# A state-space layer's weighted sums moved out of its opening, one weight split moved behind the products, and one sum moved out of the first FFN unit

## The chip, the cores and the metric

The program runs on one core of a Trainium2 chip. A core has five engines with a queue of instructions each: TensorE (PE in the profile, with its weight loads as PEld), VectorE (DVE), ScalarE (ACT), GpSimd (POOL) and SyncE (SP, which here only issues transfers). Each works its own queue in order and waits at an instruction until what it needs has been signalled. Transfers between device memory (HBM) and on-chip memory run on 16 DMA engines, and are issued from the queues of SP, ACT and POOL.

The metric is the time of one execution on the device, in microseconds (us); the figure for a kernel is the median over its runs. Before the change it is 1346.33 us.

## The reference

The model is a trunk of two layers over 512 positions of width 1024, in float32. Each layer has a token mixer and then a gated feed-forward network (FFN), both between RMS norms; a conditioning vector `c` gives each of the four sub-layers a shift, a scale and a gate (adaLN).

```python
mod = (jax.nn.silu(c) @ ada_w + ada_b).reshape(bsz, DEPTH, 2, 3, D_MODEL)
for i in range(DEPTH):
    shift, scale, gate = (mod[:, i, 0, k][:, None, :] for k in range(3))
    h = rmsnorm(x, norm_g[i, 0]) * (1.0 + scale) + shift
    y = short_conv_mixer(...) if i % 2 == 0 else ssd_mixer(...)
    x = x + gate * rmsnorm(y, norm_g[i, 1])
    shift, scale, gate = (mod[:, i, 1, k][:, None, :] for k in range(3))
    h = rmsnorm(x, norm_g[i, 2]) * (1.0 + scale) + shift
    x = x + gate * rmsnorm(swiglu_ffn(h, f_w_in[i], f_w_out[i]), norm_g[i, 3])
```

So `ada_w` is a matrix of 1024 x 12288, and `mod` is a vector of 12 pieces of 1024 numbers. A piece is needed only when its sub-layer uses it. The mixer of the second layer is a state-space layer (Mamba-2):

```python
z, xbc, dt_raw = jnp.split(h @ w_in, [M_D_INNER, M_D_INNER + M_CONV_DIM], axis=-1)
xbc = silu(causal_depthwise_conv(xbc, conv_w) + conv_b)      # x, B and C of 8 groups
dt = softplus(dt_raw + dt_bias)                              # 512 x 32 heads
cs = cumsum(dt * a)                                          # within a chunk
y = ssd_chunked(xs, dt, a, bm, cm) + d_skip * xs             # in chunks, per group
y = rms_normalize(y * silu(z), per group) * norm_g
return y @ w_out
```

## The kernel before, in words

**Number format.** TensorE is fed with pairs: a float32 weight tile is split into a rounded part (a copy on ACT) and the remainder (a subtraction on DVE, lines 230 and 231, tiles `whl`), and each product is three matmuls (lines 285 to 287). A split of a 128x1024 tile therefore costs one instruction on ACT and one on DVE, and PE can use the tile only after both.

**Order of work.** In the parts that the change touches, the order on PE, ACT and DVE is written out by hand (`tc.manual_schedule`): the instructions stand on each engine in the order in which the code issues them. In the first FFN, SP's and POOL's order is written by hand as well; in the state-space layer SP's is left to a scheduler.

**AdaLN's sums.** A piece of `mod` is summed on DVE from eight row blocks of `ada_w`: a block of 128x1024 (512 KB) is loaded into a tile `ada_st` and added to `ada_acc`, scaled by silu(c). The first block of a piece is line 125, the other seven are line 127; then line 140 folds the sum (`ada_fold`), PE adds over partitions with one small matmul (line 147, `ada_ps`), and DVE writes `mods` (line 151 and one of 156 or 158). This work is cut into steps and strewn over the program between other work. In the first FFN, `sums(n)` takes `n` steps of the three pieces that are summed there. For the last four pieces the generator `late_sums` (line 1870) yields 36 steps (eight sums and a fold, four times), and `late(n)` takes `n` of them. After each sum it issues the load of the block three further on (line 1879). `late_fin` takes a piece whose fold is done through its matmul and its last additions, one stage per call.

The tiles of these loads come from a pool `ysp` of five buffers. One holds the accumulator; one is taken in turn by `sqs`, the squares of a group's output, which PE reads at the group's end (line 1857, `ssg`); three are left for blocks that wait to be summed.

**The state-space layer** starts from PE's six leading products (`li`): the raw dt, and x, B, C and z of group 0. From the raw dt a chain runs through `dt_steps`: PE turns it (line 1618, `tokT`), DVE copies it (1619), ACT takes an exponential (1622, 1623), DVE forms softplus in fifteen small instructions (1626 to 1636), and PE forms the cumulative sums (1640, `cumT`). Behind `cumT` on PE stands everything else of the layer.

Then the groups follow. A pass of the loop `for g in range(1, NG - 1)` finishes group g (`cur`), while PE makes the products of group g + 1 (`nxt`) and the weights of group g + 2 (`nn`) are fetched. I call these passes 1 to 6, and the block ahead of them pass 0. In one pass PE does: `ssg` of the group before, two products of `nxt` (24 matmuls each, `ip`), the transposes and small products of `step_a` (`xtok`, `btokp`, `cb`), a product, the states (`st`), a product, `step_cc` (`yo`, then `yd` in two halves), and two products of z. DVE does: the head (`late_fin`, then `late`), `prev.norm` (line 1868, which needs ACT's `rg`), the taps of four convolutions (1676, three each), six weight splits (231), `step_a` (1743, 1745, 1757), the decays (1799), the chain of states `prev` (1777, 1779), and `step_cc` (1827 to 1830, for two halves). `nxt.later[i]` is a pair of functions, the ACT part and the DVE part of a weight tile's split: 0 and 1 are x, 2 is B, 3 is C, 4 and 5 are z. PE uses tile 5 in the second product of z, after `step_cc`.

PE's `yo` reads `prev`, and `st` reads `xw` (line 1743). PSUM has four `aux` banks, which `st`, `yo`, `yd`, `ssg` and the small products of `late_fin` take in turn.

**The first FFN** makes most of its inner products in 12 units (`Units`, seven quarter products per unit, tiles `sA`, `sB`, `sC` on line 654). In each unit DVE and ACT copy results out, split weights and take one step of `sums`. In the last stage of that FFN, passes `k` of a loop make plain products and take one more step each, up to `k0 + 4`.

Of the kernel before, what the change touches and what calls it, by code (L numbers as in the profile page):

```python
# [38 lines left out]
def trunk_kernel(  # L39
# [249 lines left out]
    def mm_chunk(pst, w, h, sl=FULL, ks=range(KD)):  # L289
        for k in ks:  # L290
            mm3(pst[:, sl], w, k, h[k], sl, k == 0, k == KD - 1)
# [402 lines left out]
    class Values:  # L694
# [27 lines left out]
        def sums(self, b):  # L722
            va, vb, k, (lo, hi) = self.va, self.vb[b], self.half[b], HALVES
            dve.tensor_tensor(va[:, k, hi], vb[:, :, hi], va[:, k, hi], SUB)
            dve.tensor_add(vb[:, :, hi], vb[:, :, hi], va[:, k, lo])
# [26 lines left out]
    with ExitStack() as ph:  # L752
# [582 lines left out]
        with tc.manual_schedule(engines={PE_ENGINE, mybir.EngineType.SP, mybir.EngineType.Activation,  # L1335
# [51 lines left out]
            for u in range(UN1):  # L1387
                v = u - 1
                end = u == UN1 - 1
                if not end:  # L1390
                    un.fetch(u + 2)
                else:
                    more_n = load_w([(f_w_in[0], (fu + 1) * P, P), (f_w_in[0], DFF + fu * P, P)], later=splits)
                un.product(u, "P1")
                if u:
                    un.c12(v)
                else:
                    up(3, acc[1])
                un.split_x(u + 1)
                if u:  # L1400
                    un.product(v, "P7")
                un.keep(u, "A", 0, lo_)
                un.product(u, "P5")
                if u:
                    un.c22(v)
                low_parts(1)
                un.product(u, "P2")
                un.keep(u, "C", 1, hi_)
                if u:
                    un.product(v, "P4")  # L1410
                un.c11(u)
                for step in todo:
                    next(step, None)
                sums(1)
                un.split_z(u)
                if not end:
                    un.sum_y(u + 1)
                    un.sum_s(u + 1)
                un.product(u, "P6")
                if u:  # L1420
                    un.c21(v)
                if end:
                    for op in splits[2]:
                        op()
                    more_n += load_w([(f_w_in[0], DFF + (fu + 1) * P, P)], later=splits)
                else:
                    un.split_y(u + 1)
                un.product(u, "P3")
                un.keep(u, "A", 0, hi_)
                if not end:  # L1430
                    un.split_s(u + 1)
# [53 lines left out]
            for k in range(k0, last + 1):  # L1485
                if k - k % 2 + 4 <= last:
                    load_pair_at(k - k % 2 + 4, k % 2)
                if k < k0 + 6:
                    for i in (0, 2):
                        x_load((k - k0) % 3, i + (k - k0) // 3)  # L1490
                if k in (last - 2, last - 1):
                    xy_load(n_s - 2 + k - last + 2)
                tiles[k] = in_chunk(ws[k], h)
                for step in todo:
                    next(step, None)
                q, j = divmod(k - 3, 4)
                if j < 2:
                    gate(4 + 2 * q + j, tiles[k - 1])
                else:
                    up(2 + 2 * q + j, tiles[k - 1])  # L1500
                for op in splits.get(k + 2, ()):
                    op()
                low_parts()
                sums(1 if k < k0 + 5 else 0)
                if k == 2 * NF - 12:
                    ggs.append(make_gg(1, gg_tile))
                if k == last - 1:
                    assert next(madds, 0) == 0 and not ada_sets and not quarters
                    sums_p.close()
                    ph.enter_context(tc.tile_pool(name="gap", bufs=1, side="right", reuse_waits="tile")).tile(  # L1510
                        [P, 216], F32, tag="gap", name="gap")
                    ao_p.append(ph.enter_context(tc.tile_pool(name="aop", bufs=3, side="right", reuse_waits="tile")))
                    ao_p[0].tile([P, 2, 2, 256], F32R, tag="ao", name="ao")
                    gotp = ph.enter_context(tc.tile_pool(name="gotp", bufs=1, side="right", reuse_waits="tile"))
                    c22 = gotp.tile([P, 2, T], F32, tag="c22", name="c22")
                if k >= last - 1:
                    w_prep(seq[k - last + 1])
                    a_prep(seq[k - last + 1])
# [65 lines left out]
    with ExitStack() as ph:  # L1584
# [285 lines left out]
        def late_sums():  # L1870

            uh = tmp.tile([P, 256], F32, tag="uh", name="four", bufs=2)
            sets, st = (64, 72, 80, 88), []

            def load(n):
                if n < KD * len(sets):
                    q0, k = sets[n // KD], n % KD
                    st.append(flat(ysp.tile([P, 2, T], F32, tag="ys", name="ada_st")))
                    dma(st[n], ada_w[k * P:(k + 1) * P, q0 * P:q0 * P + D])

            acc = flat(ysp.tile([P, 2, T], F32, tag="ys", name="ada_acc"))
            for n in range(3):
                load(n)
            yield uh[:, 0:P]
            for i, q0 in enumerate(sets):
                for k in range(KD):
                    ada_madd(acc, st[i * KD + k], k)
                    load(i * KD + k + 3)
                    yield
                part = uh[:, P + 32 * (i % 2):P + 32 * (i % 2) + 32]  # L1890
                ada_fold(acc, part)
                fins_late.append(late_end(q0, part))
                yield
# [8 lines left out]
        def late(n):  # L1902
            for _ in range(n):
                next(steps_late, None)
# [30 lines left out]
        with tc.manual_schedule(engines={PE_ENGINE, mybir.EngineType.Activation, mybir.EngineType.DVE}):  # L1935
            cur, nxt, nn = Group(0), Group(1), Group(2)
            nxt.weights(0)
            steps_late = late_sums()
            four = next(steps_late)
            make_four(four)  # L1940
            convs = [cur.conv(i, lead_ps[1 + i]) for i in range(4)]
            late(4)
            rest(0)
            raw = dt_raw(lead_ps[0])
            rest(1)
# [20 lines left out]
            for i in range(3):  # L1966
                next(convs[i])
            nxt.weights(1)
            mm_chunk(pz, wz1[0], h, ks=range(2, KD))
            next(convs[3])  # L1970
            for i in range(2):
# [49 lines left out]
            for g in range(1, NG - 1):  # L2021
                prev, cur, nxt = cur, nxt, nn
                nn = Group(g + 2) if g + 2 < NG else None
                nxt.e, nxt.ecs = decays(g + 1)
                conv2 = [nxt.project(i) for i in range(2)]
                prev.root()
                late_fin()
                late(4)
                nxt.later[3][0]()
                prev.norm()  # L2030
                next(conv2[0])
                next(conv2[0])
                cur.e_sub(0)
                nxt.later[3][1]()
                nxt.weights(2)
                nxt.later[4][0]()
                next(conv2[1])
                cur.e_sub(1)
                late(1)
                cur.step_a()  # L2040
                for q in range(2):
                    cur.e_exp(q)
                next(conv2[1])
                for q in range(2):
                    cur.e_mul(q)
                next(conv2[0])
                nxt.later[4][1]()
                nxt.later[5][0]()
                conv2.append(nxt.project(2))
                next(conv2[2])  # L2050
                cur.states()
                next(conv2[1])
                next(conv2[2])
                nxt.later[5][1]()
                conv2.append(nxt.project(3))
                next(conv2[3])
                next(conv2[2])
                if nn:
                    nn.weights(0)
                    nn.later[0][0]()  # L2060
                late_fin()
                cur.step_cc()
                next(conv2[3])
                if nn:
                    nn.later[0][1]()
                    nn.split(1)
                next(conv2[3])
                cur.split_sq()
                nxt.project_z(0)
                if nn:  # L2070
                    nn.weights(1)
                    nn.split(2)
                else:
                    for op in next(parts[0]):
                        op()
                nxt.project_z(1)
                cur.sums()
# [485 lines left out]
```

## Time and profile before

| what | value |
|---|---|
| median of 3 runs | 1346.33 us (1344.09 to 1349.07) |
| the profiled execution | 1343.74 us, of which the span of the profile is 1342.0 us |
| PE busy | 1309.1 us, 98% of the span |
| DVE busy | 1022.0 us, 76% |
| ACT busy | 721.3 us, 54% |
| DMA | 234.87 MB, 175 GB/s on average |

A busy share is taken over the whole program; the waits that count lie in single places. Two views matter most here: the waits (who waited for whom, how long) and the timeline of single engines. A row of the timeline gives the start in us, the time, the engine, the line, the operation, the tiles as out<-in, and in brackets the idle time before it with what ended that idle time. A matmul's time in a row reaches from its start to its end; matmuls overlap, so the pace of PE is read from the distance of two starts.

### The profile page before, as it was taken

How to read it: one execution, taken by the hardware profiler on the slowest of the kernel's cores; microseconds unless marked ns; L12 is line 12 of the kernel's file. 1: busy time of each engine (PE TensorE's matmuls, PEld its weight loads, DVE VectorE, ACT ScalarE, POOL GpSimd, SP SyncE). 2: the span in 40 equal slices, each digit the busy share in tenths (PEclk: the TensorE clock that was granted, in tenths of full speed). 3: DMA queues.
4: the chain of work that ended last, by engine and by line, in shares of the span. 5: the costliest groups of instructions: out<-in, count | busy, mean ns of one | idle time of the engine just before them, and what ended most of it. 6: DMA issues, size and time to landing. Idle time of an engine off the chain costs nothing.

```text
span 1342.0 us, 20442 instructions
## 1 busy us (share of the span) xinstructions
PE 1309.1 (98%) x7869; PEld 1150.1 (86%) x7869; DVE 1022.0 (76%) x1533; ACT 721.3 (54%) x1258; POOL 109.3 (8%) x135
## 2 busy tenths in 40 slices
PE   8999999999999999968999999999999999999998
PEld 7788889899988888867888888888789999998886
DVE  5577767888875886738889889787577777776888
ACT  5333355455423666626666677566475454554665
POOL 0000000121100320000000000000000111100330
PEclk9999999999999999988999999999999999999999
DMA  9767651799867866144654656423341888868871
GB/s 310 236 213 236 224 169 40 199 255 250 219 209 273 191 122 161 32 142 145 213 162 138 195 188 204 126 95 98 107 149 28 201 198 215 214 172 283 191 134 63
DMA packets 224277, 234.87 MB, mean 175 GB/s; under 512 B 10148, under 2 KB 176948, under 8 KB 223156
## 3 DMA queue, kind: packets, MB, share of 16 engines
q1 hardware_dynamic: 203856, 191.03, 45.9%
q0 software_dynamic: 16176, 29.63, 12.7%
q10 hardware_dynamic: 4148, 12.90, 2.9%
q8 instruction: 62, 1.02, 0.3%
q14 instruction: 35, 0.29, 0.1%
HBM read 201.66 MB, written 2.24 MB: 152 GB/s over the span
## 4 chain that ended last, share of the span: by engine, by line
PE 83%; DVE 7%; DMA 3%; ACT 3%; issue 2%; SPq 2%; DVEq 0%; ACTq 0%
PE sA L654 10%; PE ip L285 10%; PE ip L287 10%; PE ip L286 10%; PE y L387 7%; PE sC L654 5%; PE cA L2271 4%; PE cA L1310 3%; PE li L285 2%; PE li L287 2%; PE li L286 2%; PE sB L654 2%; DMA ada_st<-in_ada_w_dram 2%; PE li L936 1%; DVE whl L617 1%
## 5 line engine op out<-in xcount | busy, mean ns | idle before, releaser
L285 PE MATMUL ip<-h,whl 128*128 128x512 f32 x648 | 256.7, 396 | 0.2 <-DVE cv L1036 0.2
L287 PE MATMUL ip<-h,whl 128*128 128x512 f32 x648 | 252.9, 390 | 0.0
L286 PE MATMUL ip<-h,whl 128*128 128x512 f32 x648 | 252.8, 390 | 0.0
L285 PEld LDWEIGHTS ip<-h,whl 128*128 128x128 f32 x648 | 122.2, 189 | 26.4 <-issue 2.0
L287 PEld LDWEIGHTS ip<-h,whl 128*128 128x128 f32 x648 | 121.9, 188 | 25.8
L286 PEld LDWEIGHTS ip<-h,whl 128*128 128x128 f32 x648 | 122.2, 189 | 24.4
L654 PE MATMUL sA<-tq,whl 128*128 128x256 f32 x1008 | 131.5, 284 | 2.2 <-ACT g L664 1.2
L654 PEld LDWEIGHTS sA<-tq,whl 128*128 128x128 f32 x1008 | 125.3, 192 | 4.2 <-DVE g L681 2.1
L127 DVE SCALAR_TENSOR_TENSOR ada_acc<-ada_st,csil,ada_acc 128x1024 f32<-128x1024 f32 x70 | 89.7, 1281 | 19.2 <-DMA ada_st<-in_ada_w_dram 18.4
L231 DVE TENSOR_TENSOR whl<-wst,whl 128x1024 fp32r<-128x1024 f32 x70 | 84.8, 1219 | 22.0 <-ACT whl L230 22.0
L617 DVE TENSOR_TENSOR whl<-wsu,whl 128x1024 fp32r<-128x1024 f32 x58 | 70.8, 1221 | 33.3 <-ACT whl L616 33.3
L387 PE MATMUL y<-whlo,ys 128*128 128x512 f32 x384 | 89.3, 392 | 0.0
L387 PEld LDWEIGHTS y<-whlo,ys 128*128 128x128 f32 x384 | 71.8, 188 | 15.8 <-issue 0.6
L285 PE MATMUL li<-h,whl 128*128 128x256 f32 x288 | 83.3, 289 | 0.0
L287 PE MATMUL li<-h,whl 128*128 128x256 f32 x288 | 81.5, 283 | 0.0
L286 PE MATMUL li<-h,whl 128*128 128x256 f32 x288 | 81.4, 283 | 0.0
L230 ACT CAST whl<-wst 128x1024 fp32r<-128x1024 f32 x70 | 72.7, 1040 | 2.2 <-DMA wst<-in_m_w_in_dram 2.2
L1229 POOL DMA_DIRECT2D sg<-sg x28 | 24.6, 877 | 539.3 <-DMA sg<-in_f_w_in_dram 322.5
L616 ACT CAST whl<-wsu 128x1024 fp32r<-128x1024 f32 x58 | 60.6, 1045 | 13.3 <-PE sB L654 13.3
L1676 DVE SCALAR_TENSOR_TENSOR cu<-ip,cols,cu 128x511 f32<-128x511 f32 (+2 forms) x84 | 62.7, 746 | 3.9 <-ACT cu L1673 1.8
L2271 PE MATMUL cA<-whlo,ao 128*128 128x512 f32 x264 | 61.0, 390 | 0.4 <-DVE w2h L2478 0.2
L2271 PEld LDWEIGHTS cA<-whlo,ao 128*128 128x128 f32 x264 | 49.3, 188 | 11.6 <-ACT whlo L2236 1.2
(381 smaller groups left out, 2657.4 us busy)
## 6 DMA issues: line engine op xcount, KB each, us to landing
ada_st<-in_ada_w_dram SPq DMA_DIRECT2D x96, 512.0 KB, 6.2
wsu<-in_f_w_in_dram SPq DMA_DIRECT2D x30, 512.0 KB, 5.7
sg<-in_f_w_in_dram SPq DMA_DIRECT2D x56, 256.0 KB, 3.5
wsu<-in_f_w_in_dram SPq DMA_DIRECT2D x56, 256.0 KB, 4.8
wst<-in_m_w_in_dram SPq DMA_DIRECT2D x14, 1024.0 KB, 5.4
wst<-in_f_w_in_dram SPq DMA_DIRECT2D x10, 1024.0 KB, 6.6
wst<-in_m_w_in_dram SPq DMA_DIRECT2D x20, 512.0 KB, 5.8
wst<-in_a_w_in_dram SPq DMA_DIRECT2D x9, 1024.0 KB, 7.2
```

What stands on the lines that cost most here:

```text
L127: dve.scalar_tensor_tensor(acc, w, csil[:, k:k + 1], acc, MUL, ADD)
L230: later.append((lambda sw=sw, w=w: act.copy(w[:, 0, :nk, :], sw), lambda sw=sw, w=w: dve.tensor_tensor(w[:, 1, :nk, :], sw, w[:, 0, :nk, : ...
L231: lambda sw=sw, w=w: dve.tensor_tensor(w[:, 1, :nk, :], sw, w[:, 0, :nk, :].bitcast(F32), SUB)))
L285: pe.matmul(dst, w_at(w, 0, kk), a[:, 0, sl], start=start, stop=False)
L286: pe.matmul(dst, w_at(w, 0, kk), a[:, 1, sl], start=False, stop=False)
L287: pe.matmul(dst, w_at(w, 1, kk), a[:, 0, sl], start=False, stop=stop)
L387: pe.matmul(pst, a[:, al, tk], wt[:, wl, kk, :], start=k == 0 and i == 0, stop=k == K - 1 and i == 2, skip_group_check=bool(held))
L616: act.copy(dst[:, 0], src)
L617: dve.tensor_tensor(dst[:, 1], src, dst[:, 0].bitcast(F32), SUB)
L654: pe.matmul(dst, w[:, wl, k0 + k, :], self.moving(q, k, al), skip_group_check=True, start=q in self.FIRST and k == 0 and i == 0, stop=k == ...
L1676: dve.scalar_tensor_tensor(u[:, sft:], pst[:, :T - sft], w[3 - sft], u[:, sft:], MUL, ADD)
L2271: pe.matmul(bank[r][sub], a[:, al, q, tk], w[:, hl, q, :], start=first and k == 0, stop=last and k == 2, skip_group_check=True)
```

## The change

It has four edits, and no computation is added or removed.

1. In the state-space layer's opening, `late_sums` was started and its first four steps were taken ahead of the dt chain. Now it is started after the weights of group 1 are asked for, and `late(4)` is gone. Pass 0 keeps its two steps.
2. The heads of passes 1 to 6 take five steps in place of four. The single step in the middle of a pass is left out in passes 5 and 6. The 36 steps were 4 + 2 + 6 x 5; they are 2 + 4 x 6 + 2 x 5 now.
3. The DVE half of the split of z's second tile, `nxt.later[5][1]()`, goes from ahead of the fourth product to behind `step_cc`. With it the last taps and `split_sq` go ahead of the splits of `nn`.
4. In the first FFN, unit 0 takes no step of `sums`; the loop of the last stage takes one step more (up to `k0 + 5`).

```diff
                 for step in todo:
                     next(step, None)
-                sums(1)
+                if u:
+                    sums(1)
                 un.split_z(u)
...
-                sums(1 if k < k0 + 5 else 0)
+                sums(1 if k < k0 + 6 else 0)
...
             nxt.weights(0)
-            steps_late = late_sums()
-            four = next(steps_late)
-            make_four(four)
             convs = [cur.conv(i, lead_ps[1 + i]) for i in range(4)]
-            late(4)
             rest(0)
             raw = dt_raw(lead_ps[0])
...
             nxt.weights(1)
+            steps_late = late_sums()
+            four = next(steps_late)
+            make_four(four)
             mm_chunk(pz, wz1[0], h, ks=range(2, KD))
...
                 late_fin()
-                late(4)
+                late(5)
                 nxt.later[3][0]()
...
                 cur.e_sub(1)
-                late(1)
+                if g < 5:
+                    late(1)
                 cur.step_a()
...
                 next(conv2[2])
-                nxt.later[5][1]()
                 conv2.append(nxt.project(3))
...
                 cur.step_cc()
+                nxt.later[5][1]()
+                next(conv2[3])
+                cur.split_sq()
                 next(conv2[3])
                 if nn:
                     nn.later[0][1]()
                     nn.split(1)
-                next(conv2[3])
-                cur.split_sq()
                 nxt.project_z(0)
```

DVE at the opening of the state-space layer: `ada_acc<-ada_st` are adaLN's sums, and `dt_tok` is the dt chain's first step on DVE. Before:

```order
L213 TENSOR_TENSOR whl<-wst,whl 128x1024
L125 TENSOR_SCALAR ada_acc<-ada_st,csil 128x1024
L127 SCALAR_TENSOR_TENSOR ada_acc<-ada_st,csil,ada_acc 128x1024 x3
L1619 COPY dt_tok<-tokT 128x128
L231 TENSOR_TENSOR whl<-wst,whl 128x1024
L1626 TENSOR_SCALAR cs_tok<-ea 128x128
```

and after the change, where lines below the opening have a number higher by one:

```order
L213 TENSOR_TENSOR whl<-wst,whl 128x1024
L1620 COPY dt_tok<-tokT 128x128
L231 TENSOR_TENSOR whl<-wst,whl 128x1024
L1627 TENSOR_SCALAR cs_tok<-ea 128x128
L1628 RECIPROCAL cs_tok<-cs_tok 128x128
```

The four sums that stood ahead of the dt chain on DVE are gone from there.

DVE from the end of pass 0 into the head of pass 1 (`sqs` is the split of the squares, the two `yg` rows are `prev.norm`). Before:

```order
L1848 TENSOR_TENSOR sqs<-accg,sqs 128x512
L231 TENSOR_TENSOR whl<-wst,whl 128x1024 x2
L127 SCALAR_TENSOR_TENSOR ada_acc<-ada_st,csil,ada_acc 128x1024 x2
L140 TENSOR_REDUCE four<-ada_acc 128x32
L125 TENSOR_SCALAR ada_acc<-ada_st,csil 128x1024
L1868 SCALAR_TENSOR_TENSOR yg_6053<-yg_6053,cols_91,rg 128x512
```

and after:

```order
L1849 TENSOR_TENSOR sqs<-accg,sqs 128x512
L231 TENSOR_TENSOR whl<-wst,whl 128x1024 x2
L127 SCALAR_TENSOR_TENSOR ada_acc<-ada_st,csil,ada_acc 128x1024 x5
L1869 SCALAR_TENSOR_TENSOR yg_6041<-yg_6041,cols_91,rg 128x512
L1869 SCALAR_TENSOR_TENSOR yg_6058<-yg_6058,cols_91,rg 128x512
```

Five sums in a row now stand ahead of the norm, where two sums, a fold and a first block stood. The pieces begin four steps later, so the fold moves to the heads of passes 2, 3, 5 and 6; the head of pass 4 also has five sums in a row.

DVE around the products' sums of pass 1 (`y`, `yg` are `step_cc`'s first half). Before:

```order
L1676 SCALAR_TENSOR_TENSOR cu<-ip,cols_93,cu 128x509
L231 TENSOR_TENSOR whl<-wst,whl 128x1024
L1827 TENSOR_TENSOR y_6397<-yo,ecsb 128x384
L1828 SCALAR_TENSOR_TENSOR yg_6396<-xs_5575,dcol,yd 128x512
```

and after, from `step_cc`'s last row on:

```order
L1831 TENSOR_TENSOR yg_6403<-yg_6403,zs_6080 128x512
L231 TENSOR_TENSOR whl<-wst,whl 128x1024
L1677 SCALAR_TENSOR_TENSOR cu<-ip,cols_93,cu 128x511
L1677 SCALAR_TENSOR_TENSOR cu<-ip,cols_93,cu 128x510
L1677 SCALAR_TENSOR_TENSOR cu<-ip,cols_93,cu 128x509
L1849 TENSOR_TENSOR sqs<-accg,sqs 128x512
L231 TENSOR_TENSOR whl<-wst,whl 128x1024 x3
```

The split stands behind all eight rows of `step_cc` now, and `sqs` ahead of the three other splits.

## The prediction

> **What bounds the kernel now.** PE is busy for 98% of the span, so I read first who made PE wait. These are the only three rows of PE's waits that the change can reach (total us, times, longest):
>
> ```profile
> PE cumT L1640 <- DVE ea L1636: 17.4, 1, 17.4
> PE yd L1822 <- DVE y L1827: 1.7, 2, 1.1
> PE sA L654 <- ACT g L664: 1.2, 1, 1.2
> ```
>
> One wait of 17.4 us is more than half of PE's 33 us of idle time. The chain that ended last, from 582 us on, shows what it is made of (start, us, what):
>
> ```profile
> 582.73 0.36 PE tokT L1618 x4
> ...
> 591.94 0.34 SPq L1879
> ...
> 593.18 5.77 DMA ada_st<-in_ada_w_dram
> 599.04 1.29 DVE ada_acc L127
> ...
> 601.56 0.30 DVE dt_tok L1619
> ...
> 608.88 0.30 DVE ea L1636
> 609.32 0.77 PE cumT L1640 x2
> ...
> 642.67 1.34 PE yo L1811 x12
> 644.01 1.90 PE yd L1822 x32
> ```
>
> The raw dt is turned by 583.1 us, but its copy on DVE starts at 601.56, because the four sums stand ahead of it in DVE's queue. They wait for blocks whose loads go out only at 591.94, when PE's leading products have ended. The timeline shows both sides, and PE's pace afterwards:
>
> ```profile
> 591.63 0.28 PE L287 MATMUL li<-h,whl 128*128 128x256 f32 x1
> ...
> 595.98 0.75 DVE L125 TENSOR_SCALAR ada_acc<-ada_st,csil 128x1024 f32<-128x1024 f32 x1 [18.19 <-DMA ada_st<-in_ada_w_dram]
> ...
> 611.59 0.63 PE L285 MATMUL ip<-h,whl 128*128 128x512 f32 x1
> 612.02 0.63 PE L286 MATMUL ip<-h,whl 128*128 128x512 f32 x1
> ...
> 614.13 0.39 PE L286 MATMUL ip<-h,whl 128*128 128x512 f32 x1
> 614.36 0.39 PE L287 MATMUL ip<-h,whl 128*128 128x512 f32 x1
> ```
>
> Starts are 0.43 us apart at 612 us and 0.23 us at 614: the array is slow for a while after the gap.
>
> The passes of the group loop are the other stage. Over one pass (columns: window, its length, then busy us of PE, PEld, DVE, ACT, POOL):
>
> ```profile
> 656.80:697.10 40.30, 40.30 (x219) 33.97 (x219) 37.78 (x53) 27.24 (x46) 1.29 (x1) 1.00 0.56 179
> 697.10:738.50 41.40, 40.35 (x218) 33.73 (x217) 36.20 (x48) 26.23 (x44) 1.30 (x1) 1.00 0.57 182
> ```
>
> PE fills them; DVE is 2.5 to 5.2 us short of filling them. So what is moved into a pass is hidden only while DVE reaches each hand-over in time.
>
> **Edit 1, the opening.** DVE's copy of dt can start at 583.1 plus some 0.2 us. From that copy to `cumT` the chain above takes 609.32 - 601.56 = 7.8 us, with ACT free at that time, so `cumT` could start at 591.1. PE ends its leading products at 591.9. The whole 17.4 us goes, with 0.8 us to spare. Bounds: nothing less than none of the chain hidden, 17.4 - 7.8 = 9.6 us, and at most 17.4; I take 17.4, since each piece of the chain has its own measured row. The slow start goes with it: six large matmuls took 0.20 us too much each, and the small ones from 609.32 on some 0.8 together by the same ratio, 2.0 us in all.
>
> [...]
>
> The first three loads, SP's part of the step, now go out behind the store of the cumulative sums. Their first user is the single sum of pass 0, which PE reaches some 66 matmuls later, 15 us at 0.23; the slowest such load that I quote below took 9.8 us. So they are hidden; without that cover pass 0 would lose what is missing.
>
> **Edit 2, the heads.** Four sums of 1.28 us on DVE come back in passes 1 to 4. What counts is not their time but the loads between them. `S` is the start of `ssg`, at which PE begins a pass:
>
> ```profile
> 656.85 0.62 PE L1857 MATMUL ssg<-sqs,ones_r 128*128 128x512 f32 x2
> 659.19 2.60 DVE L127 SCALAR_TENSOR_TENSOR ada_acc<-ada_st,csil,ada_acc 128x1024 f32<-128x1024 f32 x2
> ...
> 697.10 0.62 PE L1857 MATMUL ssg<-sqs,ones_r 128*128 128x512 f32 x2
> 705.09 1.28 DVE L127 SCALAR_TENSOR_TENSOR ada_acc<-ada_st,csil,ada_acc 128x1024 f32<-128x1024 f32 x1 [4.40 <-DMA ada_st<-in_ada_w_dram]
> 706.29 1.41 DVE L1868 SCALAR_TENSOR_TENSOR yg<-yg,cols,rg 128x512 f32<-128x512 f32 x2
> 722.15 0.42 DVE L1779 TENSOR_TENSOR prev<-prev,st 128x256 f32<-128x256 f32 x1
> 722.87 1.50 PE L1811 MATMUL yo<-ct,prev 128*128 128x128 f32 x12
> 725.85 0.55 DVE L1827 TENSOR_TENSOR y<-yo,ecsb 128x384 f32<-128x384 f32 x1
> 726.45 1.09 PE L1822 MATMUL yd<-csb,xdt 128*64 128x128 f32 x16 [1.05 <-DVE y L1827]
> 730.73 2.31 DVE L1676 SCALAR_TENSOR_TENSOR cu<-ip,cols,cu 128x511 f32<-128x511 f32 x3
> ...
> 778.74 0.62 PE L1857 MATMUL ssg<-sqs,ones_r 128*128 128x512 f32 x2
> 786.99 1.28 DVE L127 SCALAR_TENSOR_TENSOR ada_acc<-ada_st,csil,ada_acc 128x1024 f32<-128x1024 f32 x1 [4.74 <-DMA ada_st<-in_ada_w_dram]
> 788.19 1.41 DVE L1868 SCALAR_TENSOR_TENSOR yg<-yg,cols,rg 128x512 f32<-128x512 f32 x2
> ```
>
> Three blocks are there when a head begins. The fourth sum's load waits for the buffer that `ssg` reads; it is there at S + 8 in pass 2 (705.09) and pass 4 (786.99), and DVE waits 4.4 and 4.7 us for it. In pass 2 the norm then starts at S + 9.2, `prev` ends at 722.57 and PE takes it at 722.87. So 0.3 us is left: a norm later than S + 9.5 makes PE wait for `yo`, us for us.
>
> A fifth sum in a row needs the load that waits for the first sum's buffer. Its measured times, in pass 1 and pass 4 (issue, and time to landing):
>
> ```profile
> 660.50 0.34 SPq L1879 DMA_DIRECT2D ada_st<-in_ada_w_dram  x1
> DMA to landing us min/median/max: 9.6/9.6/9.6
> ...
> 779.82 0.38 SPq L1879 DMA_DIRECT2D ada_st<-in_ada_w_dram  x1
> DMA to landing us min/median/max: 9.8/9.8/9.8
> ```
>
> Pass 1: the head starts as before (pass 0's DVE order ahead of it is the same), so the load lands at 670.1 = S + 13.2, the fifth sum ends at S + 14.5, and the norm is 5.0 us over the limit. Pass 4: landing at 789.6 = S + 10.9, end of the fifth sum at S + 12.2, 2.7 over. There the head begins up to a us later than now: the moved split frees a weight buffer some 6 us later, and that buffer's load and split stand ahead of the head. I take 3.2. Together 8.2 us of new waiting.
>
> Passes 2 and 5 have a fold and four blocks, pass 3 three sums, a fold and a block, pass 6 four sums and a fold: only the fourth block is waited for, and it is there at S + 8, so the norm starts near S + 9.2 and nothing is lost. The sixth step of passes 2 to 4 comes after the norm and the taps, past its load's landing. Bounds for this edit: none, if the loads land like the 5.77 us on the chain, and six passes at 5.0 = 30 us. I take 8.2, because two rows price exactly the loads that are awaited.
>
> **Edit 3, the split behind the products.** It takes 1.2 us of DVE from ahead of `step_cc`. In passes 2 and 6 PE's second half of `yd` waited for the first row of `step_cc`, the 1.7 us of the table; 1.2 us earlier in each pass covers both waits (1.05 in pass 2, the rest, 0.65, in pass 6). The split must be done by PE's second product of z, which starts one product (24 x 0.23 = 5.4 us) and `yo` and `yd` (1.34 and 1.90) behind `prev`, 8.6 us. DVE needs taps (2.3), `step_cc` (730.73 - 725.85 = 4.9) and the split (1.2), 8.4 us. Tight, but free; if it misses, a few tenths in each of six passes. Gain 1.7, bounds -2 to 1.7.
>
> **Edit 4, the first unit.** PE's 1.2 us wait there was for a copy on ACT that stood behind a split, which waited for DVE, which did this sum:
>
> ```profile
> 258.28 1.27 DVE L127 SCALAR_TENSOR_TENSOR ada_acc<-ada_st,csil,ada_acc 128x1024 f32<-128x1024 f32 x1
> 261.45 1.04 ACT L616 CAST whl<-sg 128x1024 fp32r<-128x1024 f32 x1 [4.22 <-issue]
> ...
> 434.31 1.23 DVE L1282 TENSOR_TENSOR whlo<-w2x,whlo 128x1024 fp32r<-128x1024 f32 x1 [4.21 <-ACT whlo L1281]
> ```
>
> 1.27 us less on DVE covers it: gain 1.2, at least 0. The step comes back ahead of 434 us, where DVE idles 4.2 us: nothing.
>
> **Sum.** -17.4 - 2.0 + 8.2 - 1.7 - 1.2 = -14.1 us. Against the profiled execution, 1343.74 (its span is 1342.0), 1329.6. The median of the runs stands 2.6 higher, so for a median I say 1332.
>
> **Rivals.** First, no pass gives anything back: in the new schedule the pass's loads meet other transfers and land in time. For it: the load on the chain took 5.77 us. Against: the two rows of 9.6 and 9.8 us. 1346.3 - 22.3 = 1324.
>
> Second, another wait takes the opening's place: the chain through ACT and DVE is not hidden behind the leading products, 7.8 us of it, or a late load in pass 0. For it: 0.8 us to spare is little. 1340.
>
> Third, the other side: DVE becomes the bound of the loop. The place is the head, the price up to 5.0 us in each of six passes: 30 - 22.3 gives 1354; it decides from 3.7 us per pass. For it: DVE has only 2.5 us left in pass 1. Against: four of the six heads await just one load, as three do now without PE losing more than a us.
>
> Fourth, the clock: if pass 1's 5.0 us come as one gap, PE restarts slowly, 2.0 us by the rows at 612: 1334. [...] I expect two gaps, at `st` and at `yo`.
>
> **How the numbers follow.** My forecast 0.48, the first rival 0.17, the second 0.12, the third 0.05, the fourth 0.10, the rest, unseen, 0.08. Forecast, first and fourth are faster by over 0.5% (6.7 us, about what a measurement of this kernel can tell), half of the second and of the unseen too: 0.84 faster, 0.10 within, 0.06 slower. From 1323 to 1341 all but the third and the unseen lies inside; the likeliest alone is 1328 to 1336.
>
> **What would show it.** PE's wait for `cumT` under 1 us and no 0.43 us pace behind it; PE's waits for `yo` or `st` on DVE in passes 1 and 4 alone, behind DVE waits for `ada_st` at the fifth sum; no wait of `yd`; no wait at 262 us. It is wrong if the dt chain is still late on DVE or ACT, or if passes 2, 3, 5 or 6 grow past 40.3 us.

## The result, and the profile after

The changed kernel takes 1334.49 us (median of 4 runs, 1333.14 to 1337.44) against 1345.21 us of the kernel before on the same chip: a ratio of 0.9919, 95% interval 0.9891 to 0.9948. The forecast was 1332 us, 2.5 us too fast. The profiled executions stand at 1333.14 and 1343.74 us, their spans at 1331.4 and 1342.0, 10.6 us apart where the sum said 14.1.

The opening does what the sum says. The timeline of the changed kernel there (lines below the opening have a number higher by one than before):

```profile
582.37 0.43 PE L1619 MATMUL tokT<-ident,raw 32*128 32x32 f32 x4
582.84 0.29 DVE L1620 COPY dt_tok<-tokT 128x128 f32<-128x128 f32 x1 [5.28 <-PE tokT L1619]
...
590.17 0.29 DVE L1637 SCALAR_TENSOR_TENSOR ea<-dt_tok,ea 128x128 f32<-128x128 f32 x1
...
591.35 0.28 PE L287 MATMUL li<-h,whl 128*128 128x256 f32 x1
591.47 0.39 PE L1641 MATMUL cumT<-ea,mask 128*128 128x128 f32 x2
...
637.08 0.82 PE L1858 MATMUL ssg<-sqs,ones_r 128*128 128x512 f32 x2
```

DVE's copy follows the turn of the raw dt at once, the chain is done at 590.5 us, and `cumT` follows the leading products without a gap. From `tokT` to the start of pass 1 it is 54.71 us now; before it was 656.85 - 582.66 = 74.19. That is 19.5 us.

Then half of it is given back. PE's waits on DVE now (total us, times, longest); before, there was none for `st` or `yo`, and those for `yd` and for line 681 were 1.7 us in two and 0.8 us in two:

```profile
PE st L1773 <- DVE xdt L1746: 4.0, 2, 2.7
...
PE yd L1823 <- DVE y L1828: 1.9, 4, 0.5
PE yo L1812 <- DVE prev L1780: 1.8, 4, 0.5
PE sA L654 <- DVE g L681: 1.6, 3, 0.7
```

The six passes, measured from one `ssg` to the next, took 243.25 us before and take 253.30 now. In us, for both kernels and for those of the experiments:

| kernel | pass 1 | 2 | 3 | 4 | 5 | 6 | sum |
|---|---|---|---|---|---|---|---|
| before | 40.25 | 41.39 | 40.25 | 40.01 | 40.25 | 41.10 | 243.25 |
| after | 44.97 | 41.63 | 40.73 | 43.96 | 40.37 | 41.64 | 253.30 |
| less_four | 40.82 | 41.46 | 40.25 | 40.51 | 40.26 | 41.14 | 244.44 |
| one_block | 40.02 | 40.24 | 40.14 | 40.25 | 40.25 | 40.25 | 241.15 |
| spread | 40.51 | 40.25 | 40.14 | 40.25 | 40.25 | 40.25 | 241.65 |
| mid_moved | 43.14 | 41.23 | 41.68 | 42.97 | 42.94 | 42.13 | 254.09 |
| split_back | 45.20 | 42.62 | 41.33 | 43.37 | 40.25 | 41.64 | 254.41 |
| open_back | 40.25 | 41.20 | 40.24 | 40.55 | 40.24 | 41.26 | 243.74 |
| ffn_back | 44.31 | 41.64 | 41.66 | 44.34 | 40.43 | 41.11 | 253.49 |
| spread_split_back | 40.23 | 40.78 | 40.35 | 40.93 | 40.24 | 40.26 | 242.79 |

In this loop ffn_back has the code of the changed kernel; in this one pair the sum repeats within 0.2 us, but a single pass differs by up to 0.93 us (pass 3). So a smaller change of a single pass shows nothing by itself; it needs the rows of that pass beside it. The passes in which PE never waits took 40.0 to 40.25.

Passes 1 and 4 lose 4.72 and 3.95 us. DVE's timeline at their heads and at those of passes 2 and 6, with one load of SP's, and PE behind them:

```profile
641.02 3.92 DVE L127 SCALAR_TENSOR_TENSOR ada_acc<-ada_st,csil,ada_acc 128x1024 f32<-128x1024 f32 x3
...
645.88 1.28 DVE L127 SCALAR_TENSOR_TENSOR ada_acc<-ada_st,csil,ada_acc 128x1024 f32<-128x1024 f32 x1 [0.93 <-DMA ada_st<-in_ada_w_dram]
650.59 1.28 DVE L127 SCALAR_TENSOR_TENSOR ada_acc<-ada_st,csil,ada_acc 128x1024 f32<-128x1024 f32 x1 [3.43 <-DMA ada_st<-in_ada_w_dram]
651.79 1.41 DVE L1869 SCALAR_TENSOR_TENSOR yg<-yg,cols,rg 128x512 f32<-128x512 f32 x2
...
656.48 1.27 DVE L127 SCALAR_TENSOR_TENSOR ada_acc<-ada_st,csil,ada_acc 128x1024 f32<-128x1024 f32 x1
657.67 0.68 DVE L1744 TENSOR_TENSOR xw<-xtok,dte_tok 128x512 f32<-128x512 f32 x1
...
659.10 2.05 PE L1773 MATMUL st<-xw,btok 128*128 128x256 f32 x4 [2.70 <-DVE xdt L1746]
...
681.38 0.37 SPq L221 DMA_DIRECT2D wst<-in_m_w_in_dram  x1
...
691.53 1.28 DVE L127 SCALAR_TENSOR_TENSOR ada_acc<-ada_st,csil,ada_acc 128x1024 f32<-128x1024 f32 x1 [4.09 <-DMA ada_st<-in_ada_w_dram]
692.73 1.41 DVE L1869 SCALAR_TENSOR_TENSOR yg<-yg,cols,rg 128x512 f32<-128x512 f32 x2
...
776.21 1.29 DVE L127 SCALAR_TENSOR_TENSOR ada_acc<-ada_st,csil,ada_acc 128x1024 f32<-128x1024 f32 x1 [1.42 <-DMA ada_st<-in_ada_w_dram]
777.42 1.41 DVE L1869 SCALAR_TENSOR_TENSOR yg<-yg,cols,rg 128x512 f32<-128x512 f32 x2
...
784.73 1.10 PE L1773 MATMUL st<-xw,btok 128*128 128x256 f32 x4 [1.25 <-DVE xdt L1746]
...
858.05 1.28 DVE L127 SCALAR_TENSOR_TENSOR ada_acc<-ada_st,csil,ada_acc 128x1024 f32<-128x1024 f32 x1 [4.35 <-DMA ada_st<-in_ada_w_dram]
859.37 1.25 DVE L140 TRANSPOSE_TENSOR_REDUCE four<-ada_acc 128x32 f32<-128x1024 f32 x1
860.54 1.37 DVE L1869 SCALAR_TENSOR_TENSOR yg<-yg,cols,rg 128x512 f32<-128x512 f32 x2
```

The fifth sum waits for its block, and the norm (the `yg` row) starts at S + 14.7 in pass 1 and S + 13.0 in pass 4, where S + 14.5 and S + 12.2 to 13.2 were forecast. What was not forecast: in pass 2 the norm starts at 692.73 = S + 10.7, 1.2 us past the limit of S + 9.5, and in pass 6 at 860.54 = S + 11.8. Passes 2, 3, 5 and 6 take 40.37 to 41.64 us, where the prediction had named more than 40.3 as a sign that it is wrong.

### The profile page after: what moved, and what is told of

Its sections match the earlier page's. It is cut to its first block, busy times and chain, and to the rows that moved or that the text cites. A ratio compares the mean times of both kernels' runs of the same rounds, so it can differ in the third digit from the quotient of the medians.

```text
span 1331.4 us, 20439 instructions
## 1 busy us (share of the span) xinstructions
PE 1310.1 (98%) x7869; PEld 1148.7 (86%) x7869; DVE 1022.0 (77%) x1533; ACT 723.0 (54%) x1258; POOL 109.8 (8%) x135
## 4 chain that ended last, share of the span: by engine, by line
PE 75%; DVE 10%; DMA 9%; ACT 4%; issue 2%; SPq 0%; ACTq 0%; DVEq 0%; POOLq 0%
PE sA L654 10%; PE y L387 8%; PE ip L285 7%; PE ip L287 7%; PE ip L286 7%; PE sC L654 5%; PE cA L2272 4%; DMA ada_st<-in_ada_w_dram 4%; PE cA L1310 3%; PE sB L654 2%; PE li L936 2%; PE li L285 2%; PE li L287 2%; PE li L286 2%; DVE cu L1677 2%; DMA wsu<-wsu 2%
## 5 line engine op out<-in xcount | busy, mean ns | idle before, releaser
L616 ACT CAST whl<-wsu 128x1024 fp32r<-128x1024 f32 x58 | 60.7, 1046 | 14.5 <-PE sB L654 12.2
```

The costliest lines, as they stand in the source:

```text
L616: act.copy(dst[:, 0], src)
```

## The experiments

The theory to test: the price of edit 2 is the wait for loads in the heads, not DVE's work. The rival is a DVE that is simply full. Beside these stand two smaller questions, what edits 3 and 4 are worth.

**less_four.** Four of the 36 steps, four sums with their loads, are left out, so that heads of four suffice.

```diff
+            todo = [(q0, k) for i, q0 in enumerate(sets) for k in range(KD if i else 4)]
...
-                for k in range(KD):
+                for k in range(KD if i else 4):
...
-                late(5)
+                late(4)
...
-                if g < 5:
-                    late(1)
+                late(1)
                 cur.step_a()
```

> The changed kernel with four sums and four loads left out (the first of the four late pieces is summed from four of its eight row blocks), and heads of four steps again with the single step in every pass. Theory (the fifth sum in a row waits for a load): passes 1 and 4 of the group loop lose their new waits and fall from 45.0 and 44.0 us to 40.3 each, the other passes stay within 0.5 us, so the profiled time falls by about 8.7 us, from 1333.1 to about 1324.5. Rival (DVE is simply full, each further sum costs its own 1.28 us): four sums fewer give 4 x 1.28 = 5.1 us, 1328, spread over passes 1 to 4. Rival (the moved split delays loads and so every head): passes 2, 3 and 6 keep the 0.2 to 0.5 us that they are longer than before.

Measured: 1325.0 us (ratio to before 0.9861, 0.9844 to 0.9877), profiled at 1324.51. Pass 1 falls by 4.15 us and pass 4 by 3.45, 7.6 of the 8.9 in all. The gain sits in these two passes and not in passes 1 to 4 alike, as four equal prices of 1.28 us would have it; but less work and fewer waits go together here, so it takes the next run to part them. The other rival, the moved split, shows in the rows and not in the time: passes 2, 3 and 6 are back at 41.46, 40.25 and 41.14 us, near the kernel before, yet the fourth sum of pass 2 still starts at S + 9.2 and not at S + 8.0. What the split costs there it gives back at `yd`, where PE waits 0.5 us in place of 1.05, and 0.3 for `yo`.

**one_block.** All 32 sums read one block; 31 loads are left out, DVE's instructions stay.

```diff
-                if n < KD * len(sets):
+                if n == 0:
...
-                    ada_madd(acc, st[i * KD + k], k)
-                    load(i * KD + k + 3)
+                    ada_madd(acc, st[0], k)
                     yield
```

> The changed kernel in which all 32 sums of the late pieces read one block that is loaded once; the other 31 loads of 512 KB are left out, DVE's instructions and their order are the same. Theory (the heads' cost is the wait for loads, not DVE's work): DVE waits for no block, the norm starts near S + 9 in passes 1 and 4, passes 1 to 6 take 40.0 to 40.4 us each, and the time falls by about 10 us to 1323. Rival (DVE is full): five sums and the single one still stand ahead of the states' inputs, passes 1 and 4 stay above 42 us, and the time is 1329 or more.

Measured: 1321.31 us (0.9831, 0.9816 to 0.9845). The windows of pass 1, of this kernel and of the changed one (window, its length, then busy us of PE, PEld, DVE, ACT, POOL, the granted clock, DMA share, GB/s):

```profile
636.92:676.94 40.02, 40.02 (x217) 33.74 (x215) 38.22 (x48) 27.41 (x46) 1.48 (x1) 1.00 0.41 119
```

```profile
637.08:682.05 44.97, 42.27 (x217) 34.78 (x215) 38.29 (x49) 29.30 (x48) 1.48 (x1) 0.96 0.54 176
```

DVE works 38.2 us in the one and 38.3 in the other, and PE loses 5 us only in the kernel that waits for blocks. DVE is not full; the loads are the price. This is the first rival's case, nothing given back. With 31 loads fewer the DMA engines also move less (119 against 176 GB/s), so the next run keeps all loads.

**spread.** Nothing is left out. The head takes the three sums whose blocks are there; the others go behind the norm.

```diff
                 late_fin()
-                late(5)
+                late(3)
...
-                if g < 5:
-                    late(1)
+                late(2)
                 cur.step_a()
+                if g < 5:
+                    late(1)
```

> The changed kernel with three sums in each head, as many as there are blocks, two in place of the single one in the middle of a pass, and in passes 1 to 4 a third behind the first rows that make the states' inputs. Nothing is left out. Theory (loads): the norm starts near S + 6.5, the later sums find their blocks landed, no wait of PE for the states or the sums of products is left, passes 1 to 6 take 40.0 to 40.4 us, and the time is 1321 to 1324. Rival (DVE is full): six sums in a pass still cost, passes 1 and 4 stay above 42 us, 1329 or more. Rival (loads late wherever they stand): DVE waits for blocks in the middle of the pass, and PE waits there as it did.

Measured: 1322.1 us (1321.5 to 1323.12; ratio to before 0.9838, 0.9823 to 0.9852), and the fastest here that leaves nothing out. Against the changed kernel it gains 12.4 us by the medians and 11.3 by the profiled executions; the kernels before that were run beside the two stand 1.5 us apart, so the smaller figure is the safer. The loop gains 11.65. DVE in pass 1, which starts at 636.94:

```profile
640.69 3.92 DVE L127 SCALAR_TENSOR_TENSOR ada_acc<-ada_st,csil,ada_acc 128x1024 f32<-128x1024 f32 x3
644.52 1.41 DVE L1869 SCALAR_TENSOR_TENSOR yg<-yg,cols,rg 128x512 f32<-128x512 f32 x2
...
649.21 1.28 DVE L127 SCALAR_TENSOR_TENSOR ada_acc<-ada_st,csil,ada_acc 128x1024 f32<-128x1024 f32 x1
650.72 1.28 DVE L127 SCALAR_TENSOR_TENSOR ada_acc<-ada_st,csil,ada_acc 128x1024 f32<-128x1024 f32 x1 [0.23 <-DMA ada_st<-in_ada_w_dram]
651.92 0.68 DVE L1744 TENSOR_TENSOR xw<-xtok,dte_tok 128x512 f32<-128x512 f32 x1
```

The norm starts at S + 7.6, the taps and a split pass the time in which the blocks land, the wait for a block is 0.23 us, and `xw` comes 5.6 us earlier in the pass than in the changed kernel (S + 15.0 against S + 20.6). Only a single wait of 0.2 us for `yo` is left in the loop.

**mid_moved.** Heads of five stay; the single step of passes 1 and 4 goes to the pass's end.

```diff
-                if g < 5:
+                if g in (2, 3):
                     late(1)
                 cur.step_a()
...
                 cur.split_sq()
+                if g in (1, 4):
+                    late(1)
```

> The changed kernel with the single step of passes 1 and 4 moved from ahead of the states' inputs to behind the split of the squares, near the end of the pass; heads of five stay. Theory: in pass 1 the states' inputs come 1.27 us earlier, PE's gap falls from 2.7 to about 1.4 us, the clock isn't halved behind it, and PE then waits for the chain of states instead, so pass 1 gains 1.3 to 2.9 us and pass 4 about 1.2: 1329 to 1331. Rival (only the wait for the load counts, the single step is hidden): passes 1 and 4 stay at 45.0 and 44.0 us. Rival (the half clock at 659 us has nothing to do with the gap): the states' matmuls of pass 1 take 2.0 us in place of 1.0 with the shorter gap as well.

Measured: 1333.7 us (0.9927, 0.9912 to 0.9942), no better than the changed kernel. Passes 1 and 4 gained 1.8 and 1.0 us, about as expected, so the single step was not hidden; the gap in pass 1 fell to 1.14 us, and the states' matmuls there took 1.10 us, as they do in split_back at a granted clock of 1.00 (2.05 us in the changed kernel, at 0.50). The forecast of 1329 to 1331 missed all the same: pass 5 lost 2.57 us. (Pass 3 is 0.95 us longer as well, but it takes 41.66 us in ffn_back too, which has the changed kernel's loop.) SP's and DVE's timeline about the start of pass 5 (805.94 in mid_moved, 808.37 in the changed kernel), first of mid_moved:

```profile
803.45 0.34 SPq L1880 DMA_DIRECT2D ada_st<-in_ada_w_dram  x1
805.72 0.37 SPq L221 DMA_DIRECT2D wst<-in_m_w_in_dram  x1
806.59 5.89 SPq L1880 DMA_DIRECT2D ada_st<-in_ada_w_dram  x4
...
817.79 1.28 DVE L127 SCALAR_TENSOR_TENSOR ada_acc<-ada_st,csil,ada_acc 128x1024 f32<-128x1024 f32 x1 [5.66 <-DMA ada_st<-in_ada_w_dram]
```

```profile
809.02 5.06 SPq L1880 DMA_DIRECT2D ada_st<-in_ada_w_dram  x4
...
817.65 1.28 DVE L127 SCALAR_TENSOR_TENSOR ada_acc<-ada_st,csil,ada_acc 128x1024 f32<-128x1024 f32 x1 [3.93 <-DMA ada_st<-in_ada_w_dram]
```

The fourth block's load goes out 0.65 us into the pass in both (806.59 and 809.02), but its sum starts 11.2 us later here and 8.6 there. What is new is the load at 803.45: the moved sum sets its buffer free at the end of the pass, and the load that follows stands ahead of the block that the next head awaits. The weights' load moves with it, from S - 1.4 to S - 0.2 (805.72), so these rows do not tell the two apart. Either way, a step has two ends that count, when its block is there and when the load behind it goes out.

**split_back.** Edit 3 undone in the changed kernel.

```diff
                 next(conv2[2])
+                nxt.later[5][1]()
                 conv2.append(nxt.project(3))
...
                 cur.step_cc()
-                nxt.later[5][1]()
-                next(conv2[3])
-                cur.split_sq()
                 next(conv2[3])
                 if nn:
                     nn.later[0][1]()
                     nn.split(1)
+                next(conv2[3])
+                cur.split_sq()
```

> The changed kernel with edit 3 undone: the DVE half of the split of z's second tile stands ahead of the fourth product again. The prediction gave edit 3 a gain of 1.7 us, the waits for yd: by it this run takes 1335, with waits of about 1 us for yd in passes 2 and 6. Theory after the result: the moved split frees its weight buffer later, the loads of the next weights and of the fourth block go out about 1 us later, so the heads of passes 2 to 6 are about 1 us later than with the split in its old place, and edit 3 gains nothing on balance: undone, the fourth block lands near S + 8 again, passes 3 and 5 take 40.3 us, passes 2 and 6 41.4 and 41.1, pass 4 about 43, pass 1 stays at 45, and the time is 1331.

Measured: 1334.25 us (0.9931, 0.9917 to 0.9946), the same as the changed kernel within the measurement; the loop's sum is 1.1 us longer. PE's waits:

```profile
PE yd L1823 <- DVE y L1828: 5.4, 4, 1.6
PE st L1773 <- DVE xdt L1746: 3.1, 1, 3.1
...
PE yo L1812 <- DVE prev L1780: 2.2, 5, 0.7
```

My expectation of 1331 missed. Its half about the loads holds: the fourth sum starts at S + 8.4, 7.4, 7.7 and 8.2 in passes 3 to 6, against 9.0, 9.1, 9.3 and 9.3 with edit 3. But `step_cc` is late by the split again, and the waits for `yd` grow from 1.9 to 5.4 us. By the loop's sums edit 3 helps by 1.1 us in these heads, too little for the medians to show.

**open_back.** Edits 3 and 4 alone.

```diff
             nxt.weights(0)
+            steps_late = late_sums()
+            four = next(steps_late)
+            make_four(four)
             convs = [cur.conv(i, lead_ps[1 + i]) for i in range(4)]
+            late(4)
...
-                late(5)
+                late(4)
...
-                if g < 5:
-                    late(1)
+                late(1)
```

> Edits 3 and 4 alone: the first four sums stand in the opening again and the heads have four steps. By the prediction's terms 1343.7 - 1.7 - 1.2 = 1340.8, with the 17.4 us wait for cumT and the slow pace behind it back. Theory after the result: edit 3 gains nothing, so 1342.5, passes 2 and 6 stay 0.5 to 1 us over 40.3 us. Rival (the opening's sums are not what cumT waited for): the wait stays gone, 1325 or less.

Measured: 1344.18 us against 1343.7 before (ratio 1.0006, 0.9996 to 1.0015): no change. The wait for `cumT` is back with 17.8 us, so the four sums are its cause. Both forecasts of the time, 1340.8 and 1342.5, missed: edits 3 and 4 alone gain nothing that the medians show. The loop's sum is 0.5 us above that of before. At the start of pass 2 the rows of SP and DVE of open_back (the pass starts at 696.95) and then of before (697.10; the sum itself stands in the prediction, at 705.09):

```profile
695.99 0.37 SPq L221 DMA_DIRECT2D wst<-in_m_w_in_dram  x1
697.59 0.34 SPq L1880 DMA_DIRECT2D ada_st<-in_ada_w_dram  x1
...
705.88 1.28 DVE L127 SCALAR_TENSOR_TENSOR ada_acc<-ada_st,csil,ada_acc 128x1024 f32<-128x1024 f32 x1 [3.85 <-DMA ada_st<-in_ada_w_dram]
```

```profile
694.34 0.37 SPq L221 DMA_DIRECT2D wst<-in_m_w_in_dram  x1
697.74 0.82 SPq L1879 DMA_DIRECT2D ada_st<-in_ada_w_dram  x2
```

The moved split lets the weights' load go out 1.65 us later by the clock, 1.8 us later in its pass, so it stands right ahead of the fourth block's. That block's own load goes out as early as ever (0.64 us into the pass in both), and its sum starts at S + 8.9 instead of S + 8.0; passes 4 and 6 show 9.0 and 9.0 against 8.2 and 7.8. So in pass 2 the sum is 0.9 us later behind a weights' load that is 1.8 us later. How the one load delays the other is not shown: no run here parts waiting behind it from sharing the DMA engines with it.

**ffn_back.** Edit 4 undone in the changed kernel.

```diff
-                if u:
-                    sums(1)
+                sums(1)
...
-                sums(1 if k < k0 + 6 else 0)
+                sums(1 if k < k0 + 5 else 0)
```

> The changed kernel with edit 4 undone: unit 0 of the first FFN takes its sum again. By the prediction's term PE's wait of 1.2 us near 262 us is back and the time is 1334.3; the window from 250 to 300 us shows 1.2 us more idle time of PE. Rival (the gain of edit 4 was lost to a later wait of the same FFN, the 0.65 us one between 350 and 400 us): that wait goes with the edit, and the time changes by 0.5 us or less.

Measured: 1334.96 us (0.9932, 0.9917 to 0.9947), not told from the changed kernel's. PE's busy time in two windows (columns as above), first of ffn_back, then of the changed kernel:

```profile
250.00:300.00 50.00, 48.17 (x386) 47.08 (x385) 41.67 (x57) 25.11 (x42) 8.19 (x10) 1.00 0.93 242
350.00:400.00 50.00, 49.91 (x327) 45.64 (x326) 38.31 (x51) 19.60 (x32) 2.61 (x3) 1.00 0.74 213
```

```profile
250.00:300.00 50.00, 49.36 (x395) 48.20 (x394) 41.66 (x58) 25.50 (x43) 8.65 (x11) 1.00 0.92 239
350.00:400.00 50.00, 49.26 (x320) 44.97 (x319) 37.47 (x49) 18.59 (x30) 2.60 (x3) 1.00 0.75 216
```

The edit gains 1.19 us in the first window and loses 0.65 in the second, 0.54 on balance. So both the prediction's gain and the rival's later wait are there. All the kernels agree: the wait near 263 us stands in the one before and in ffn_back alone, the one near 370 us in the eight others. The timeline of the changed kernel shows what came into the second:

```profile
359.51 0.68 DVE L151 TENSOR_TENSOR mods<-ada_ps,cols 32x8 f32<-32x8 f32 x4
360.22 0.17 DVE L158 TENSOR_TENSOR gcol<-mods,cols 128x8 f32<-128x8 f32 x1
...
370.09 3.13 PE L654 MATMUL sA<-tq,whl 128*128 128x256 f32 x24 [0.74 <-DVE g L681]
```

All steps between unit 0 and the last stage come one unit later. With them the end of a piece, 0.8 us on DVE, moves from 350.5 us in the kernel before to 359.5, into the next unit. That this unit has no room for it is read from the wait behind it; no run moves the piece's end alone.

**spread_split_back.** The version spread with edit 3 undone, by the lines shown at split_back.

> The version with three sums in the heads and three strewn behind them, with edit 3 undone as well. Theory: with the heads short, DVE reaches the chain of states some 3 us early, the split in its old place finds room, and PE waits for nothing more: passes of 40.1 to 40.5 us and 1322, the same as with edit 3. Rival (edit 3 is needed for yd): waits of about 1 us for yd come back in some of six passes, 1324 or more.

Measured: 1323.6 us (0.9847, 0.983 to 0.9863) against 1322.1; the loop's sum is 242.79 against 241.65. Waits for `yd` of 0.31 and 0.43 us are back in passes 2 and 4. That lies between the two expectations: the waits come back, as the rival said, but smaller than its 1 us. So edit 3 is worth about 1 us here too, near what a profile can tell.

## Why the prediction was right or wrong

| term | predicted | measured |
|---|---|---|
| opening, wait and slow restart | -19.4 | -19.48 |
| passes 1 and 4 | +8.2 | +8.67 |
| passes 2, 3, 5 and 6 | -1.7 | +1.38 |
| edit 4 | -1.2 | -0.54 |
| start of the program and behind pass 6 | 0 | -0.63 |
| sum | -14.1 | -10.6 |

**Edit 1** was right in size and in mechanism: the chain was ready before the leading products ended, as forecast (its last row on DVE ends at 590.46 us, and `cumT` could start at 591.1 by the forecast), so `cumT` starts right behind them, at 591.47. Open_back brings the wait back. The 2.0 us of the slow restart were right as well: the granted clock of the kernel before is 0.50 until 613.34 us, 4.0 us after PE restarts at 609.32, which at half speed costs 2.0. The first loads at 594.81 us cost pass 0 nothing. The second rival did not come.

**Edit 2** was right in mechanism for passes 1 and 4: the fifth sum waits for its block. In pass 4 the row was the right price (a load of 10.1 us where 9.8 was taken). In pass 1 the size was luck: the head began 1.6 us later than I took it to, at S + 3.9, and the load took 8.2 us in place of 9.6, so the block landed at S + 13.4 where S + 13.2 was forecast; why the head began later is not shown. Of the places where the wait would show, I named `st` and `yo`; pass 1 has `st` alone, pass 4 both, and `yo` came in passes 2 and 6 too.

**The step that failed** is that passes 2, 3, 5 and 6 lose nothing, because the fourth block "is there at S + 8". The four passes were to gain the 1.7 us of edit 3 and lost 1.4: with 3.1 us this row is most of what separates the forecast from the result. I read S + 8 from passes in which the weights' load went out 2.8 us ahead of the pass. Edit 3 moves that load to 0.7 to 1.4 us ahead, and the fourth sum starts at S + 9.0 to 9.5 (in pass 2 the load goes out at 681.38, S - 0.7, and the sum starts at 691.53, S + 9.5). I had the later load in the prediction, but only as a later start of pass 4's head. In pass 6 the forecast also left out the fold, 1.25 us, which stands behind the fourth sum and ahead of the norm. How far the norm stood past its limit accounts for the passes to within 0.5 us. The limit is S + 9.5; in passes 5 and 6, without the single step, it lies 1.27 us later, S + 10.8:

| pass | norm at S + | past the limit | over 40.25 us |
|---|---|---|---|
| 1 | 14.7 | 5.2 | 4.7 |
| 2 | 10.7 | 1.2 | 1.4 |
| 3 | 9.6 | 0.1 | 0.5 |
| 4 | 13.0 | 3.5 | 3.7 |
| 5 | 10.5 | -0.3 | 0.1 |
| 6 | 11.8 | 1.0 | 1.4 |

**Edit 3** was priced on one side alone. The split does free 1.2 us ahead of `step_cc`; the later load takes 0.6 to 1.7 us in the heads. By the loop's sums, each of one execution, it gains 1.1 us where heads are late and loses 0.5 alone (open_back). Nor did the waits for `yd` vanish: wherever PE waits for `prev`, DVE still has 2.3 us of taps to do before `step_cc`, and PE waits the 0.5 us for `yd` as well.

**Edit 4** gained what was forecast in its unit (1.19 us against 1.2), but the other end was wrong: the sentence looked only at where the one step comes back, not at the pieces' ends, which move with the steps.

**The rivals.** A full DVE (the third) is excluded by one_block and spread. The time of the fourth, 1334, was met, but by luck: the gap in pass 1 did come as one, of 2.7 us, and the clock did fall to 0.50 behind it, but that cost little (below). The chances add up to 0.85 for faster, not 0.84. The first is what spread reaches by another order.

The last line of the table holds what no edit reaches: the first FFN's products begin 0.25 us later in this execution (253.03 against 252.78 us), and behind pass 6 two short waits for ACT's `xn`, 0.83 us together, are absent. Both differ among the kernels that have the same code there.

## What to carry to other kernels

In this loop work that reads prefetched blocks cost the wait for its loads (pass 1 took 44.97 us, and 40.02 in one_block with the same work of DVE): put as many pieces in a row as there are blocks in the buffers, and the rest where a load's time has passed since a buffer came free (here from 1334.5 to 1322.1 us, with nothing left out). When work is moved, follow both ends of each buffer it holds: moving a consumer later moves the next load of that buffer, which may then stand ahead of another that someone awaits. When a step is taken out of a sequence, look at every later step that shifts with it, the odd ones above all.

## What was not expected of the hardware

PE's clock fell after a gap shorter than one that left it alone. The granted clock, as a share of full speed, is the third column from the end in these windows of the changed kernel, behind the gap of 2.70 us in pass 1 (656.4 to 659.1):

```profile
656.40:658.70 2.30, 0.00 (x0) 0.00 (x0) 2.30 (x4) 2.29 (x4) 0.00 (x0) 1.00 0.32 47
...
658.90:659.10 0.20, 0.00 (x0) 0.03 (x1) 0.20 (x2) 0.20 (x1) 0.00 (x0) 0.50 0.98 338
659.10:661.80 2.70, 2.70 (x7) 2.17 (x8) 2.66 (x5) 0.41 (x2) 0.00 (x0) 0.50 0.86 301
...
662.40:663.00 0.60, 0.60 (x5) 0.47 (x4) 0.60 (x2) 0.26 (x1) 0.00 (x0) 1.00 0.00 0
```

and of split_back, behind a gap of 3.11 us at the same place:

```profile
655.90:659.00 3.10, 0.02 (x1) 0.00 (x0) 3.10 (x5) 3.09 (x4) 0.00 (x0) 1.00 0.39 83
659.00:660.00 1.00, 0.96 (x5) 0.89 (x6) 1.00 (x3) 0.07 (x1) 0.00 (x0) 1.00 1.04 364
```

In ffn_back the clock was halved as well behind a gap of 2.33 us (0.50 from 660 to 662 us). Behind 1.25 us in pass 4 of the changed kernel it stayed at 1.00 (784.7 to 788 us), and behind 1.14 us in mid_moved the states' matmuls took 1.10 us. The half clock lasts from 658.86 to 662.27 us, 3.41 us, and in ffn_back about 3.4 us too; behind the 17.4 us gap of the kernel before it lasts from 596.27 to 613.34, 17.07 us, which is five times 3.41. Why 2.33 and 2.70 us of gap were enough where 3.11 us were not is not shown: no run here varies the gap alone.

The half clock cost almost nothing: the states' matmuls took 2.05 us in place of 1.10, yet pass 1 is as long in split_back, at a clock of 1.00 there, as in the changed kernel (45.20 and 44.97 us). There PE merely reached `yo` earlier and waited for DVE's `prev` (2.2 us in five waits over the loop, against 1.8 in four).
